# Placing the latent-attention products, four kept partial sums and the weight order of the gated output stage in a decoder block

## The chip, the core and the metric

One Trainium2 chip, one core of it. The metric is device time in microseconds of one execution: the median of the runs, beside one execution that the hardware profiler recorded. Engines are named as the profile names them: PE (TensorE, matrix products), PEld (its weight loads), DVE (VectorE), ACT (ScalarE), POOL (GpSimd), SP (the queue from which nearly all transfers are issued).

## The reference

One layer of a decoder block, batch 1, 1024 positions, width 1024, float32. Cut to what matters here:

```python
h    = rmsnorm(x, mix_norm_g)
proj = h @ w_in   # -> qa, ka, va (sliding window), q_lat (384), kv_lat (256), k_r (32), g_a, g_b (1024 each)
o_a  = swa_sink_attention(rope(qa), rope(ka), va, sinks)        # 8 heads of 64, window 128
qb   = rmsnorm(q_lat) @ w_uq      # 8 heads x (64 nope + 32 rope)
kvb  = rmsnorm(kv_lat) @ w_ukv    # 8 heads x (64 k_nope + 64 v)
o_b  = causal_softmax((q_nope k_nope' + rope(q_rope) rope(k_r)') * 96**-0.5) @ v
y    = sigmoid(g_a) * (o_a @ w_o_swa) + sigmoid(g_b) * (o_b @ w_o_mla)
x    = x + y @ w_out
x    = x + (silu(h2 @ w_gate) * (h2 @ w_up)) @ w_down           # h2 = rmsnorm(x)
out  = rmsnorm(x)
```

## The kernel before

Every matrix product is kept exact to nearly float32 by three products of two halves: an operand is split into a high part and the rest (`split`, L161: ACT copies the high part, DVE or POOL subtracts to get the low part), and `mm3` (L168) issues high·high, high·low, low·high at L172, L173 and L174. In the profile most matmuls therefore carry one of these three lines and most splits L163 (ACT) and L166 (DVE), so one goes by tile names.

The program has these stages: input projection and sliding-window attention with the gate products (`gate_step`) between, until about 347 us; then the **product stage** (loop at L1290), which makes from the latents `cq` and `ckv` the queries (`prod_q`, `prod_rope`), keys (`prod_k`) and values (`prod_v`) of the eight latent-attention heads; then the **head loop** over 64 steps t (L1326), eight heads of eight query blocks; then the **output stage** (`mix_b`, loop at L1394); then the product with `w_out` (tile `xo`, L1579) and the feed-forward part.

*Product stage.* For j in 0..3 it computes two 512-wide halves of `prod_k(j)` (6 matmuls each, heads 2j and 2j+1), for j<2 `prod_rope(j)` (18 matmuls, tiles `qr`, `qrs`), two halves of `prod_q(j)` (9 each) and two `prod_v` (6 each): 204 matmuls. Keys and queries are split, stored to DRAM (`kn_d`, `qn_d`, `qr_d`) and loaded again per head into the tiles `kT` (three of them, `load_k`, L1135) and `qT` (`load_q`, L1138), since a head's 64 rows and its rope rows have to lie in one tile of 96 partitions. Scores of steps 0 and 1 are issued within j = 3 (L1308, L1312).

*Head loop.* At step t the program issues `scores(t+2)` (PE products into a PSUM tile `scb`, DVE mask and row minimum at L1175, ACT exponential at L1176 into `p`, POOL reciprocal and scaling at L1177 and L1178), then the products with the values that are due (`pv`, L1214 and L1215, from three steps after their transposes on), then from t = 9 on a piece of the sliding-window output product `mix_a` (`fill`, L1321: 4 pieces of 6 matmuls in a head, tile `oA`), then `transposes(t)` (L1192, tile `pTb`, split into `pth` and `ptl`). Beside that, `split_oa` (L1236) splits the sliding-window output (`oar`) in steps 0 to 7. `mix_a(dc)` (L1253) leaves its 128 rows of `o_a @ w_o_swa` in a tile `ar`, stores it to `ar_d` and drops it (L1265 to L1267).

*Output stage.* For each of eight 128-row blocks dc of y: `load_sigs(dc)` loads two gate tiles (`sg`) and `ar`; `sigmoids` on ACT (L1248); `mix_b` (L1367): POOL multiplies `ar` by its gate (L1374), PE computes two halves of `o_b @ w_o_mla` (24 matmuls, tile `oB`), DVE multiplies them by the other gate (L1379), DVE adds one half and POOL the other (L1382, shown as L180), and `split` writes `yh` and `yl`. The weights `("ob", i)` serve the blocks 2i and 2i+1. They are loaded (`st.load_to`) before block 2i-2 and split into `wh`, `wl` (`st.conv_to`) after `mix_b` of block 2i-1, that is just ahead of their use:

```python
    for dc in range(8):
        ...
        if dc % 2 == 0 and dc < 6:
            st.load_to(st.index[("ob", dc // 2 + 1)])
        ...
        mix_b(dc)
        if dc % 2 == 1 and dc < 6:
            st.conv_to(st.index[("ob", dc // 2 + 1)])
```

*What sets the order.* From L1039 to L1557 nothing is ordered by hand: a planner in the compiler takes the instructions by program order as their priority, puts each engine's into one fixed list by its own cost estimates and reuses tile slots as they come free. Each engine and each queue then works its list in order; a waiting instruction holds all behind it. Tiles come from 21 slots "u" (4 KB per partition), 17 slots "v" (8 KB) and eight PSUM banks: four tiles `P1` and, in the other four banks, tiles `PX` (four of 512 columns, or two of 1024 in the head loop).

Of the kernel before, what the change touches and what calls it, by code (L numbers as in the profile page):

```python
# [8 lines left out]
F32 = mybir.dt.float32  # L9
F32R = mybir.dt.float32r  # L10
# [7 lines left out]
P = 128  # L18
# [71 lines left out]
def hybrid_block_kernel(  # L90
# [53 lines left out]
    def U(name, dt=F32, shape=(P, 1024)):  # L144
        return pool.tile(list(shape), dt, tag="u", name=uid(name))
# [7 lines left out]
    def P1(name, shape=(P, 512)):  # L153
        return ps1.tile(list(shape), F32, tag="ps", name=uid(name))
# [6 lines left out]
    def split(hi, lo, src, eng=None):  # L161

        i = nc.scalar.copy(hi, src)  # L163
        if held[0]:
            tc.keep_in_program_order(i)
        (eng or nc.vector).tensor_tensor(lo, src, hi.bitcast(F32), op=ALU.subtract)  # L166
# [18 lines left out]
    def half(s):  # L185
        return slice(512 * s, 512 * s + 512)
# [23 lines left out]
    ar_d = dram.tile([8, P, S], F32, name="ar_d")  # L210
# [87 lines left out]
    uq_unit(2)  # L298
    for dp in range(4):
        plain(("oa", dp), w_o_swa[dp], (P, 4, 256), True)  # L300
    for dp in range(4):
        plain(("ob", dp), w_o_mla[dp], (P, 4, 256))
    for r, hf in enumerate((0, 1, 0)):
        for j in range(4):
# [783 lines left out]
    wuq = st.get(("uq", 1)) + st.get(("uq", 2))  # L1088

    vM = []  # L1090
    qT = {}
    mask = U("mask")
    cos_t, sin_t = rope_t

    def prod_rope(s):
        ps = [P1("q") for _ in range(2)]
        for w, p in zip(w_rope, ps):
            mm3(p, [((w[:, 0, k], w[:, 1, k]), (cq[k][0][:, half(s)], cq[k][1][:, half(s)])) for k in range(3)])
        c, d = U("qr", F32, (P, 2, 512)), U("qr", F32, (P, 2, 512))
        for i in range(2):  # L1100
            nc.vector.tensor_tensor(c[:, i], ps[i], cos_t[:, half(s)], op=ALU.mult)
            nc.vector.tensor_tensor(d[:, 1 - i], ps[i], sin_t[:, half(s)], op=ALU.mult)
        sub(c[:, 0], c[:, 0], d[:, 0], nc.gpsimd)
        add(c[:, 1], c[:, 1], d[:, 1], nc.gpsimd)
        for i in range(2):
            t = U("qrs", F32R, (P, 2, 512))
            split(t[:, 0], t[:, 1], c[:, i], nc.gpsimd)
            nc.sync.dma_start(qr_d[i][:, :, half(s)], t.bitcast(F32))

    def prod_q(j, s):  # L1110
        w = wuq[j]
        ps = P1("q")
        mm3(ps, [((w[:, 0, k], w[:, 1, k]), (cq[k][0][:, half(s)], cq[k][1][:, half(s)])) for k in range(3)])
        t = U("qns", F32R, (P, 2, 512))
        nc.scalar.activation(t[:, 0], ps, AF.Copy, scale=-SC_B)
        nc.vector.scalar_tensor_tensor(t[:, 1], ps, -SC_B, t[:, 0].bitcast(F32), op0=ALU.mult, op1=ALU.subtract)
        nc.sync.dma_start(qn_d[j][:, :, half(s)], t.bitcast(F32))

    def prod_k(j, s):
        ps = P1("k")  # L1120
        mm3(ps, [((wk[0][:, k, blk(j)], wk[1][:, k, blk(j)]), (ckv[k][0][:, half(s)], ckv[k][1][:, half(s)]))
                 for k in range(2)])
        t = U("kns", F32R, (P, 2, 512))
        split(t[:, 0], t[:, 1], ps)
        nc.sync.dma_start(kn_d[j][:, :, half(s)], t.bitcast(F32))
# [10 lines left out]
        nc.sync.dma_start(kT[h % 3][0:64].bitcast(F32), kn_d[h // 2, 64 * (h % 2):64 * (h % 2) + 64])  # L1136

    def load_q(h):  # L1138
        t = qT[h] = V("qT", F32R, (P, 2, S))
        nc.sync.dma_start(t[0:64].bitcast(F32), qn_d[h // 2, 64 * (h % 2):64 * (h % 2) + 64])  # L1140
# [139 lines left out]

    wo = {}
    NT = NH * NB

    def load_sigs(dc):
        for i in (dc, 8 + dc):
            load_sig(i)
        ar[dc] = U("ar")
        nc.sync.dma_start(ar[dc], ar_d[dc])

    for j in range(4):  # L1290
        prod_k(j, 0)
        prod_k(j, 1)
        if j < 2:
            prod_rope(j)
        if j == 2:
            nc.vector.memset(mask[:, 0:S - P], 0.0)
            nc.vector.tensor_scalar(mask[:, S - P:], band[:, P:], -1.0, None, op0=ALU.mult)
        prod_q(j, 0)
        if j == 1:
            load_k(0)  # L1300
        if j == 2:
            load_k(1)
            load_q(0)
        if j == 3:
            load_k(2)
            load_q(1)
            psum_phase("psb", 2)
            scores(0)  # L1308
        prod_q(j, 1)
        prod_v(2 * j)  # L1310
        if j == 3:
            scores(1)  # L1312
        prod_v(2 * j + 1)
        if j == 1:
            for g in range(2):
                load_oa(g, 0)
        if j == 3:
            for g in range(2):
                load_oa(g, 1)
    st.load_to(st.index[("oa", 0)])  # L1320
    fill = {}  # L1321
    for i in range(16 - 2):
        for c in range(2):
# [2 lines left out]
    for t in range(NT):  # L1326
        h, n = divmod(t, NB)
        if t + 2 < NT:
            scores(t + 2)
        while pvq and pvq[0][0] <= t:  # L1330
            pv(*pvq.pop(0)[1:])
        if n == 2 and h + 2 < NH:
            load_q(h + 2)
        if n == 6 and h + 3 < NH:
            load_k(h + 3)
        hh, nn = step(t)
        if nn % 2 == 1:
            pvq.append((t + 3, hh, nn // 2))
        e = t - (NT - 8)
        if e == 6:  # L1340
            psum_phase("psc", 4)
        if t in fill:
            dc, sh, c0 = fill[t]
            mix_a(dc, sh, c0, 2, P1("oA") if c0 == 0 else None)
        transposes(t)
        held[0] = True
        if t < 8:
            split_oa(t % 4 // 2, t // 4, t % 2)
        if t == 4:
            st.conv_to(st.index[("oa", 0)])  # L1350
        if n in (0, 4) and h in (2, 4, 6):
            (st.load_to if n == 0 else st.conv_to)(st.index[("oa", h // 2)])
        if e == 4:
            load_sigs(0)
# [9 lines left out]
    for r in rest[1:]:  # L1364
        mix_a(*r, 0, 4, PX("oA"))

    def mix_b(dc):  # L1367
        if dc % 2 == 0:
            wo["b"] = st.get(("ob", dc // 2))
        w = wo["b"]  # L1370
        ga, gb = gate.pop(dc), gate.pop(8 + dc)
        a_ = ar.pop(dc)
        for sh in range(2):
            nc.gpsimd.tensor_tensor(ga[:, half(sh)], a_[:, half(sh)], ga[:, half(sh)], op=ALU.mult)  # L1374
        for sh in range(2):
            cs = half(sh)
            pb = PX("oB")
            mm3(pb, [((w[0][:, c, blk(dc % 2)], w[1][:, c, blk(dc % 2)]), obT[(c, sh)]) for c in range(4)])
            nc.vector.tensor_tensor(gb[:, cs], pb, gb[:, cs], op=ALU.mult)  # L1379
        for sh in range(2):  # L1380
            cs = half(sh)
            add(ga[:, cs], ga[:, cs], gb[:, cs], (nc.vector, nc.gpsimd)[sh * (dc < 7)])  # L1382
# [11 lines left out]
    for dc in range(8):  # L1394
        if dc + 2 < 8:
            load_sigs(dc + 2)
        if dc % 2 == 0 and dc < 6:
            st.load_to(st.index[("ob", dc // 2 + 1)])
        if dc + 1 < 8:
            sigmoids(dc + 1)  # L1400
        mix_b(dc)
        if dc % 2 == 1 and dc < 6:
            st.conv_to(st.index[("ob", dc // 2 + 1)])
        if dc >= 4:
            st.load_to(st.index[("out", 0, dc - 4)])
        if dc >= 5:
            st.conv_to(st.index[("out", 0, dc - 5)])
    st.conv_to(st.index[("out", 0, 3)])


# [149 lines left out]
    for seg, (sh, hf) in enumerate(((0, 0), (0, 1), (1, 1), (1, 0))):  # L1560
# [6 lines left out]
        for b in range(4 * sh, 4 * sh + 4):  # L1567
# [256 lines left out]
```

## Time and profile before

| | us |
|---|---|
| median of 3 runs (1368.16 to 1372.61) | 1369.6 |
| the profiled execution, whole | 1365.05 |
| its span, first to last instruction | 1363.2 |
| PE busy (modelled, matmuls overlap) | 1332.9 |
| DVE / ACT / POOL busy | 898.6 / 634.7 / 577.9 |
| mean granted PE clock | 0.991 |
| moved by the transfers | 232.01 MB, 170 GB/s |

A line of the time view reads: start, duration, engine, line of the kernel, operation, output tile <- input tiles, shape, and in brackets how long the engine was idle ahead of it and what ended that. A line of the stage view ("windows") gives for each engine the busy time in a stretch with the number of instructions, then the granted PE clock (1.00 is full), the mean busy share of the 16 DMA engines and their rate.

### The profile page before, as it was taken

Reading aid. Unit: us, or ns where it says so; the run is one execution under the profiler, and the core shown is the slowest. Engines: PE = TensorE matmul, PEld = TensorE weight load, DVE = VectorE, ACT = ScalarE, POOL = GpSimd, SP = SyncE. Lnnn points to the kernel's source line nnn. Section 1 sums busy time; section 2 is a strip of 40 time slices with the busy share of each in tenths; the row PEclk is TensorE's granted clock in tenths of the full one; section 3 lists DMA queues with packets and bytes.
Section 4 is the critical chain, followed back from the end, with each engine's and each line's share of the span. In section 5 each row is a group of like instructions: output and inputs, shape, how many; then the busy total and the mean of one; then the engine's idle time right before and its main releaser. Section 6 shows DMA issues by size and latency. Waiting matters only on the chain.

```text
span 1363.2 us, 19047 instructions
## 1 busy us (share of the span) xinstructions
PE 1332.9 (98%) x6564; PEld 1120.6 (82%) x6564; DVE 898.6 (66%) x1458; ACT 634.7 (47%) x1289; POOL 577.9 (42%) x621
## 2 busy tenths in 40 slices
PE   9999999999989999988999999999999999999997
PEld 6899878878878988867887888888888888888886
DVE  7868777776657667656448956666556654664862
ACT  7435666675346667744326323223222332644443
POOL 2126546452225554462031465766665551022421
PEclk9999999999999999989999999999999999999999
DMA  9464322335695431492243344654444525996504
GB/s 370 150 194 154 117 96 77 120 104 189 226 331 134 94 86 48 174 388 101 82 196 132 116 173 144 232 185 164 149 152 162 175 81 182 378 383 244 170 11 144
DMA packets 87873, 232.01 MB, mean 170 GB/s; under 512 B 9889, under 2 KB 16545, under 8 KB 86433
## 3 DMA queue, kind: packets, MB, share of 16 engines
q1 hardware_dynamic: 86336, 228.43, 48.4%
q10 hardware_dynamic: 1440, 2.36, 0.5%
q8 instruction: 52, 0.85, 0.3%
q14 instruction: 45, 0.36, 0.1%
HBM read 155.92 MB, written 74.32 MB: 169 GB/s over the span
## 4 chain that ended last, share of the span: by engine, by line
PE 86%; DVE 4%; issue 3%; POOL 3%; ACT 2%; DMA 1%; POOLq 0%; ACTq 0%; DVEq 0%
PE fa L174 7%; PE fa L172 7%; PE fa L173 7%; PE fb L174 6%; PE fb L172 6%; PE fb L173 6%; PE fd L172 5%; PE fd L174 5%; PE fd L173 5%; PE xo L173 2%; PE xo L174 2%; PE pTb L1192 2%; PE xo L172 2%; PE ob L1215 1%; PE ob L1214 1%
## 5 line engine op out<-in xcount | busy, mean ns | idle before, releaser
L166 DVE TENSOR_TENSOR wl<-wr,wl 128x512 fp32r<-128x512 f32 x150 | 151.9, 1037 | 72.1 <-ACT wl L163 71.8
L166 DVE TENSOR_TENSOR lrv<-lr,lrv 128x1024 fp32r<-128x1024 f32 x77 | 105.1, 1396 | 48.9 <-ACT lrv L163 45.0
L163 ACT CAST lrv<-lr 128x1024 fp32r<-128x1024 f32 x77 | 80.2, 1052 | 95.7 <-PE fd L174 59.5
L172 PE MATMUL fd<-lrv 128*128 128x512 f32 x308 | 119.8, 389 | 0.0
L173 PE MATMUL fd<-lrv 128*128 128x512 f32 x308 | 119.8, 389 | 0.0
L174 PE MATMUL fd<-lrv 128*128 128x512 f32 x308 | 119.8, 389 | 0.0
L177 POOL TENSOR_TENSOR wr<-wr,sm 128x512 f32<-128x512 f32 (+1 forms) x38 | 46.3, 1228 | 148.9 <-DVE wl L166 116.6
L163 ACT CAST wl<-wr 128x512 fp32r<-128x512 f32 x150 | 86.8, 622 | 1.4 <-DVE wr L831 1.2
L166 DVE TENSOR_TENSOR wl<-sm,wl 128x512 fp32r<-128x512 f32 x60 | 49.2, 846 | 46.4 <-ACT wl L163 46.3
L1177 POOL TENSOR_TENSOR denb<-denb,neg_one 128x1 f32<-128x1 f32 x64 | 39.2, 612 | 93.0 <-ACT p L1176 88.1
L310 POOL TENSOR_SCALAR ms<-ss 128x1 f32<-128x1 f32 x32 | 8.4, 263 | 144.3 <-ACT xn L1586 67.7
L174 PEld LDWEIGHTS fd<-lrv 128*128 128x128 f32 x308 | 57.8, 188 | 12.1
L173 PEld LDWEIGHTS fd<-lrv 128*128 128x128 f32 x308 | 57.8, 188 | 12.1
L172 PEld LDWEIGHTS fd<-lrv 128*128 128x128 f32 x308 | 57.8, 188 | 11.8
L1176 ACT ACTIVATE p<-scb,nmb 128x384 f32<-128x384 f32 (+3 forms) x64 | 47.8, 746 | 39.5 <-DVE nmb L1175 35.4
L166 DVE TENSOR_TENSOR ptl<-pTb,pth 128x512 fp32r<-128x512 f32 (+2 forms) x96 | 50.6, 553 | 22.1 <-ACT pth L163 21.4
L1175 DVE CUSTOM_DVE_ANT_0 scb<-scb,mask 128x384 f32<-128x384 f32 (+3 forms) x64 | 48.6, 761 | 17.9 <-PE scb L1167 15.9
L1478 ACT ACTIVATE act<-sm 128x512 f32<-128x512 f32 x11 | 7.0, 633 | 104.9 <-DVE sm L180 104.9
L1178 POOL TENSOR_SCALAR p<-p,denb 128x384 f32<-128x384 f32 (+3 forms) x64 | 49.1, 768 | 6.3
L172 PE MATMUL xo<-wv,yh 128*128 128x512 f32 x120 | 47.4, 395 | 2.2 <-ACT wv L163 2.2
L173 PE MATMUL xo<-wv,yh 128*128 128x512 f32 x120 | 46.8, 390 | 1.7 <-DVE wv L166 1.7
L1192 PE MATMUL pTb<-ident,p 128*128 128x128 f32 x288 | 43.8, 279 | 3.9 <-POOL p L1178 3.8
(352 smaller groups left out, 4296.8 us busy)
## 6 DMA issues: line engine op xcount, KB each, us to landing
lr<-la_d SPq DMA_DIRECT2D x77, 256.0 KB, 5.4
wr<-in_w_gate_dram SPq DMA_DIRECT2D x22, 512.0 KB, 4.1
wr<-in_w_up_dram SPq DMA_DIRECT2D x22, 512.0 KB, 5.2
wd<-in_w_down_dram SPq DMA_DIRECT2D x22, 512.0 KB, 6.8
rb_d<-wd SPq DMA_DIRECT2D x22, 512.0 KB, 2.7
la_d<-sd SPq DMA_DIRECT2D x22, 512.0 KB, 4.8
lr<-rb_d SPq DMA_DIRECT2D x44, 256.0 KB, 5.4
lr<-in_w_down_dram SPq DMA_DIRECT2D x33, 256.0 KB, 5.6
```

The source lines that it names most:

```text
L163: i = nc.scalar.copy(hi, src)
L166: (eng or nc.vector).tensor_tensor(lo, src, hi.bitcast(F32), op=ALU.subtract)
L172: nc.tensor.matmul(ps, ah, bh, start=first and i == 0, stop=False, skip_group_check=go_on)
L173: nc.tensor.matmul(ps, ah, bl, start=False, stop=False, skip_group_check=go_on)
L174: nc.tensor.matmul(ps, al, bh, start=False, stop=last and i == n - 1, skip_group_check=go_on)
L177: eng.tensor_tensor(out, a, b, op=ALU.subtract)
L1175: nc.vector.tensor_tensor_reduce(s_, s_, m_, 1.0, -NEG, op0=ALU.add, op1=ALU.min, accum_out=nm)
L1176: nc.scalar.activation(p_, s_, AF.Exp, scale=-1.0, bias=nm, accum_out=den)
L1177: nc.gpsimd.tensor_tensor(den, den, neg_one[:, 0:1], op=ALU.pow)
L1178: nc.gpsimd.tensor_scalar(p[:, 0:w], p[:, 0:w], den, 0.0, op0=ALU.mult, op1=ALU.add)
L1192: nc.tensor.transpose(pp[:, i], p[:, blk(k0 + i)], ident)
L1214: nc.tensor.matmul(po[:, q_off:], vst, hi[:, kb % 4, q_off:], start=kb == 0, stop=False)
```

## The change

Four parts.

1. The product stage is written out in another order. `prod_k(0)`, both `prod_rope`, `prod_q(0)`, `prod_k(1)`, `prod_q(1)` and the values come first, then `prod_k(2)`, `prod_q(2,0)`, `scores(0)`, `prod_q(2,1)`, a value block, `scores(1)`, two value blocks. `prod_k(3)` and `prod_q(3)` (30 matmuls) go into steps 0, 1, 2, 3, 5 and 6 of the head loop (`first`). Keys and queries of heads 0 and 1 are written by ACT and DVE straight into `kT` and `qT` in two pieces of 64 partitions, not through DRAM. `prod_rope` splits in place and stores high and low parts; it and `prod_q(0)`, `prod_q(1)` use the `PX` banks.
2. `load_oa`, the load of the first `w_o_swa` unit, its split and `split_oa` move into the steps 1 to 11 of the head loop.
3. `mix_a` of blocks 4 to 7 leaves its result in two "v" tiles that stay until the output stage; `ar_d` holds only blocks 0 to 3.
4. The output stage takes the blocks in the order 4, 0, 5, 1, 6, 2, 3, 7 and the `("ob", i)` units in the order 2, 0, 3, 1, two at a time; the first two are loaded in the last head. The `w_out` units are loaded one block earlier in the loop, and the `xo` product adds up its eight parts in a matching order.

The diff, cut:

```diff
     def prod_q(j, s, k0=0, n=3):
...
+        outs = [(t[:, 0], t[:, 1], ps)] if j else [
+            (qT[u][0:64, 0, half(s)], qT[u][0:64, 1, half(s)], ps[64 * u:64 * u + 64]) for u in range(2)]
...
     def prod_k(j, s):
...
+        if j == 0:
+            for u in range(2):
+                split(kT[u][0:64, 0, half(s)], kT[u][0:64, 1, half(s)], ps[64 * u:64 * u + 64])
+            return
...
     def mix_a(dc, sh, c0, n, ps=None):
...
-            ar[dc] = U("ar")
+            if dc < 4:
+                ar[dc] = U("ar")
+            elif dc % 2 == 0:
+                t = V("ar", F32, (P, 2, S))
+                ar[dc], ar[dc + 1] = t[:, 0], t[:, 1]
...
-            if sh == 1:
+            if sh == 1 and dc < 4:
                 nc.sync.dma_start(ar_d[dc], ar.pop(dc))
...
+    DCS = (4, 0, 5, 1, 6, 2, 3, 7)
...
+    prod_k(2, 0)
+    prod_k(2, 1)
+    prod_v(4)
+    load_k(2)
+    prod_q(2, 0)
+    psum_phase("psb", 2)
+    scores(0)
+    prod_q(2, 1)
+    prod_v(5)
+    scores(1)
+    prod_v(6)
+    prod_v(7)
+    first = {0: lambda: prod_k(3, 0), 1: lambda: prod_k(3, 1), 2: lambda: prod_q(3, 0, 0, 2),
+             3: lambda: prod_q(3, 0, 2, 1), 5: lambda: prod_q(3, 1, 0, 2), 6: lambda: prod_q(3, 1, 2, 1)}
...
+        if t in first:
+            first[t]()
...
-        if t < 8:
-            split_oa(t % 4 // 2, t // 4, t % 2)
-        if t == 4:
+        if t in (1, 5):
+            for g in range(2):
+                load_oa(g, t // 4)
+        if t == 3:
+            st.load_to(st.index[("oa", 0)])
+        if 4 <= t < 12:
+            split_oa(t % 4 // 2, t // 4 - 1, t % 2)
+        if t == 7:
             st.conv_to(st.index[("oa", 0)])
...
+        if e in (2, 6):
+            st.load_to(st.index[("ob", 2 if e == 2 else 0)])
         if e == 6:
-            st.conv_to(st.index[("ob", 0)])
+            st.conv_to(st.index[("ob", 2)])
...
+    sigmoids(DCS[0])
+    st.conv_to(st.index[("ob", 0)])
     new_quads("y")
+    for i, dc in enumerate(DCS):
+        if i in (1, 2):
+            st.load_to(st.index[("ob", (3, 1)[i - 1])])
+        if 3 <= i < 7:
+            st.load_to(st.index[("out", 0, i - 3)])
+        if i + 2 < 8:
+            load_sigs(DCS[i + 2])
+        if i + 1 < 8:
+            sigmoids(DCS[i + 1])
+        mix_b(dc, i)
+        if i in (2, 3):
+            st.conv_to(st.index[("ob", (3, 1)[i - 2])])
+        if i >= 4:
+            st.conv_to(st.index[("out", 0, i - 4)])
...
-            mm3(ps, [(hT(k, blk(b)), (wo2[k // 2][0][:, k % 2], wo2[k // 2][1][:, k % 2])) for k in range(NK)])
+            mm3(ps, [(hT(k, blk(b)), (wo2[k // 2][0][:, k % 2], wo2[k // 2][1][:, k % 2])) for k in (0, 1, 4, 5, 2, 6, 3, 7)])
```

More of the change, by code (lines that the diff above doesn't have):

```diff
@@ L1090, in hybrid_block_kernel @@
     vM = []
-    qT = {}
+    qT = {h: V("qT", F32R, (P, 2, S)) for h in range(2)}
     mask = U("mask")
@@ L1105, in prod_rope, with prod_q @@
         for i in range(2):
[L1106 to L1110, printed above, removed]
-        w = wuq[j]
[L1112 to L1117, printed above, removed]
+            split(d[:, i].bitcast(F32R), c[:, i].bitcast(F32R), c[:, i], nc.gpsimd)
+        for i, t in enumerate((d, c)):
+            nc.sync.dma_start(qr_d[:, :, i, half(s)].rearrange("a p c -> p a c"), t)
+    q_ps = {}
+    def prod_q(j, s, k0=0, n=3):
+        w = wuq[j]
+        if k0 == 0:
+            q_ps[0] = (P1 if j > 1 else PX)("q")
+        ps = q_ps[0]
+        mm3(ps, [((w[:, 0, k], w[:, 1, k]), (cq[k][0][:, half(s)], cq[k][1][:, half(s)])) for k in range(k0, k0 + n)],
+            k0 == 0, k0 + n == 3)
+        if k0 + n < 3:
+            return
+        t = U("qns", F32R, (P, 2, 512)) if j else None
+        outs = [(t[:, 0], t[:, 1], ps)] if j else [
+            (qT[u][0:64, 0, half(s)], qT[u][0:64, 1, half(s)], ps[64 * u:64 * u + 64]) for u in range(2)]
+        for hi, lo, src in outs:
+            nc.scalar.activation(hi, src, AF.Copy, scale=-SC_B)
+            nc.vector.scalar_tensor_tensor(lo, src, -SC_B, hi.bitcast(F32), op0=ALU.mult, op1=ALU.subtract)
+        if j:
+            nc.sync.dma_start(qn_d[j][:, :, half(s)], t.bitcast(F32))
     def prod_k(j, s):
@@ L1286, in load_sigs @@
             load_sig(i)
[L1287 to L1320, printed above, removed]
+        if dc < 4:
+            ar[dc] = U("ar")
+            nc.sync.dma_start(ar[dc], ar_d[dc])
+    prod_k(0, 0)
+    prod_k(0, 1)
+    prod_rope(0)
+    prod_rope(1)
+    prod_q(0, 0)
+    prod_q(0, 1)
+    prod_v(0)
+    load_q(0)
+    load_q(1)
+    prod_k(1, 0)
+    prod_k(1, 1)
+    prod_q(1, 0)
+    prod_q(1, 1)
+    prod_v(1)
+    prod_v(2)
+    prod_v(3)
+    nc.vector.memset(mask[:, 0:S - P], 0.0)
+    nc.vector.tensor_scalar(mask[:, S - P:], band[:, P:], -1.0, None, op0=ALU.mult)
+    prod_k(2, 0)
[12 more added lines that the diff above has]
+             3: lambda: prod_q(3, 0, 2, 1), 5: lambda: prod_q(3, 1, 0, 2), 6: lambda: prod_q(3, 1, 2, 1)}
     fill = {}
@@ L1387, in sigmoids @@
             sigmoid(i)
-    load_sigs(1)
+    load_sigs(DCS[1])
     split_ob(3, 0)
     split_ob(3, 1)
-    sigmoids(0)
+    sigmoids(DCS[0])
+    st.conv_to(st.index[("ob", 0)])
     new_quads("y")
[L1394 to L1407, printed above, removed]
+    for i, dc in enumerate(DCS):
[12 more added lines that the diff above has]
+            st.conv_to(st.index[("out", 0, i - 4)])
     st.conv_to(st.index[("out", 0, 3)])
```

23 lines of the change are left out of this document (13 added, 10 removed).

## The prediction

> **What bounds the kernel now.** I read the page first, then the busy times by stage, then the time view of PE wherever a stage showed PE short of full, then the other engines there.
>
> ```profile
> span 1363.2 us, 19047 instructions
> PE 1332.9 (98%) x6564; PEld 1120.6 (82%) x6564; DVE 898.6 (66%) x1458; ACT 634.7 (47%) x1289; POOL 577.9 (42%) x621
> ```
>
> PE is the bound, so a change pays only where PE is idle or slowed. The stages show where that is (start and end, then per engine busy us, PE clock, transfer share):
>
> ```profile
> 347.00:394.00 47.00, 46.90 (x206) 38.19 (x204) 22.03 (x35) 14.75 (x27) 10.17 (x8) 1.00 0.81 259
> 394.00:402.00 8.00, 5.71 (x28) 4.28 (x28) 5.50 (x12) 4.78 (x11) 3.27 (x6) 1.00 1.07 347
> 402.00:410.00 8.00, 6.64 (x32) 6.35 (x32) 6.92 (x16) 5.98 (x14) 4.71 (x7) 0.58 1.03 324
> 410.00:422.00 12.00, 9.95 (x65) 8.50 (x64) 10.19 (x22) 8.66 (x20) 7.25 (x8) 0.99 0.96 211
> 422.00:442.00 20.00, 20.00 (x135) 18.18 (x134) 13.84 (x32) 13.61 (x32) 10.22 (x17) 1.00 0.31 90
> ...
> 581.00:595.00 14.00, 8.08 (x21) 5.67 (x20) 6.83 (x7) 7.47 (x9) 10.95 (x8) 0.63 1.02 410
> 595.00:613.00 18.00, 17.84 (x79) 14.37 (x77) 11.18 (x13) 7.58 (x10) 9.99 (x7) 1.00 0.98 370
> 613.00:622.00 9.00, 5.03 (x14) 3.43 (x13) 7.42 (x8) 6.02 (x8) 4.42 (x3) 0.81 0.84 292
> ```
>
> Two places leak. The first head (394 to 422) loses 2.29 + 1.36 + 2.05 = 5.7 us of idle time, and 6.64 x 0.42 = 2.8 us to the clock of 0.58: **8.5 us**. The later heads (422 to 442) lose nothing. The product stage ahead (347 to 394) is full on PE. The output stage leaks from 581 to 622; its loss is counted below. The change touches just these places.
>
> **Part 1: products into the first head.** PE's gaps there, in the time view (in brackets the idle time and its end):
>
> ```profile
> 347.20 0.39 PE L172 MATMUL k<-ckv,wv 128*128 128x512 f32 x1
> ...
> 358.08 0.39 PE L172 MATMUL v<-wv,ckv 128*128 128x512 f32 x1
> ...
> 394.87 0.41 PE L1165 MATMUL scb<-kT,qT 96*128 96x384 f32 x1 [0.93 <-DMA qT<-qr_d]
> ...
> 397.05 0.50 PE L1165 MATMUL scb<-kT,qT 96*128 96x512 f32 x1 [0.72 <-ACT p L1176]
> ...
> 402.72 1.22 PE L1192 MATMUL pTb<-ident,p 128*128 128x128 f32 x7 [1.20 <-POOL p L1178]
> ...
> 417.66 0.66 PE L1192 MATMUL pTb<-ident,p 128*128 128x128 f32 x4 [1.93 <-POOL p L1178]
> ...
> 421.89 0.40 PE L172 MATMUL oA<-wv,wv 128*128 128x512 f32 x1
> ```
>
> From the first row to the second lie 48 matmuls (12 for keys, 36 for queries): 10.88 / 48 = **0.2267 us** each. The gaps end on softmax (ACT, POOL): a step of the first head has too little PE work to cover that latency, for no `mix_a` piece and few `pv` are due. The change puts 30 x 0.2267 = 6.8 us of products there, taken from a stage where each costs its full time. If they filled idle time only, and the clock held, the head would give back its 8.5 us; nothing else there can be gained. Against that stand lumps: `prod_k(3)` comes as 1.36 us in one step, and steps 4 and 7 get none. I keep one gap of the size of the 417.66 row, 2.0 us, and take **6.5**; the ends are 8.5 and, if the products only push softmax back, 0.
>
> The splits on DVE and ACT (mean ns after the busy time):
>
> ```profile
> L166 DVE TENSOR_TENSOR wv<-oar,wv 128x512 fp32r<-128x512 f32 x8 | 6.2, 774 | 0.2
> L163 ACT CAST wv<-oar 128x512 fp32r<-128x512 f32 x8 | 5.1, 636 | 0.0
> L166 DVE TENSOR_TENSOR vM<-v,vM 128x512 fp32r<-128x512 f32 x2 | 1.3, 684 | 0.0
> L163 ACT CAST vM<-v 128x512 fp32r<-128x512 f32 x2 | 1.1, 604 | 0.0
> ```
>
> Four product splits enter the head, 4 x (0.68 + 0.60) = 5.1 us; four of the eight `split_oa` leave it for steps 8 to 11, 4 x (0.77 + 0.64) = 5.6 us. That cancels; in the next head DVE is at 13.84 of 20 us and takes 4 x 0.77. Writing heads 0 and 1 in 64-row pieces adds four splits, again 5.1 us, in the product stage, where DVE is busy 22 of 47 us and ACT 15: cost 0 under PE; 5.1 at most without that cover. Moving load and split of the `w_o_swa` unit costs 0 by the same slack.
>
> Scores(0) comes earlier: 147 matmuls precede it in program order, 347.2 + 147 x 0.2267 = 380.5. Its keys and plain queries are then in place; its rope rows still go through DRAM:
>
> ```profile
> 358.25 2.55 POOL L166 TENSOR_TENSOR qrs<-qr,qrs 128x512 fp32r<-128x512 f32 x2 [0.73 <-ACT qrs L163]
> ```
> ```profile
> qr_d<-qrs SPq DMA_DIRECT2D x4, 512.0 KB, 3.1
> ...
> qT<-qr_d SPq DMA_DIRECT2D x9, 128.0 KB, 10.6
> ```
>
> The first rope half is done at 360.8 as now; the second, directly behind it on POOL, needs four such operations (5.1 us): 366. Store 3.1, issue about 2, load 10.6: 382, 1.5 us behind scores(0). The load is queued on SP after both stores, ahead of the stores of `prod_k(1)` and `prod_q(1)`, whose readers come heads later. 27 matmuls (6.1 us) stand between and behind scores(0) and scores(1), which the planner can put first. Cost 0; without that cover 1.5.
>
> **Part 2: the output stage.**
>
> ```profile
> 570.26 0.39 PE L172 MATMUL oB<-obT,wh 128*128 128x512 f32 x1
> ...
> 586.04 0.79 PE L172 MATMUL oB<-obT,wh 128*128 128x512 f32 x1 [4.74 <-ACT wh L163]
> ...
> 588.45 0.79 PE L174 MATMUL oB<-obT,wl 128*128 128x512 f32 x1 [1.19 <-DVE wl L166]
> ...
> 615.51 0.50 PE L172 MATMUL xo<-wv,yh 128*128 128x512 f32 x1 [2.23 <-ACT wv L163]
> 617.76 0.50 PE L173 MATMUL xo<-wv,yh 128*128 128x512 f32 x1 [1.74 <-DVE wv L166]
> ...
> 621.80 0.39 PE L172 MATMUL xo<-wv,yh 128*128 128x512 f32 x1
> ...
> 631.12 0.39 PE L173 MATMUL xo<-wv,yh 128*128 128x512 f32 x1
> ```
>
> Between the first and the last row lie 8 x 24 = 192 `oB` matmuls and four of `xo` (the first at 615.51, the last at 621.80): 196 x 0.2267 = 44.4 of 60.9 us. **16.4 us** are lost, idle time and the slow clock after it. What the 586.04 row waited for, on DVE, POOL, ACT, ACT, DVE:
>
> ```profile
> 581.76 0.68 DVE L1379 TENSOR_TENSOR sg<-oB,sg 128x512 f32<-128x512 f32 x1
> 582.61 1.78 POOL L180 TENSOR_TENSOR sg<-sg,sg 128x512 f32<-128x512 f32 x1 [1.32 <-ACT yh L163]
> 584.42 0.62 ACT L163 CAST yh<-sg 128x512 fp32r<-128x512 f32 x1 [0.92 <-POOL sg L180]
> 584.95 1.04 ACT L163 CAST wh<-wr 128x1024 fp32r<-128x1024 f32 x1
> 586.09 2.30 DVE L166 TENSOR_TENSOR wl<-wr,wh 128x1024 fp32r<-128x1024 f32 x1
> 601.29 1.22 DVE L166 TENSOR_TENSOR wl<-wr,wh 128x1024 fp32r<-128x1024 f32 x1
> ```
>
> The weight split ran on ACT without idle time ahead of it: it had not waited for its transfer but in line, behind the end of block 1, which itself follows PE's last matmul. So PE stood still for a whole chain: DVE, POOL, ACT, then the split. The change puts one block (24 x 0.2267 = 5.44 us of PE) between that split and its use. PE ended at 586.04 - 4.74 = 581.30; the high half was there at 585.99, 4.7 us later, the low half at 588.39, 7.1 later, or 6.0 with the 1.22 us of the 601.29 row. PE now wants them after 5.44 and, for the third matmul, 5.9. So the high half is in time and the low half 0.1 to 1.2 us late, for units 3 and 1: 0.2 to 2.4, I take 1.2. At the end, the new order of `xo` wants the last `w_out` unit after 15 matmuls (3.4 us) instead of 18; if its split stays behind block 7's chain (4.7) it is 1.3 late; I take 1.2. Gain 16.4 - 2.4 = **14.0**; the ends are 16.4 and 7 (below, second rival).
>
> [...]
>
> Transfers: sixteen of 512 KB are dropped (for each of `kn_d` and `qn_d` two stores and two loads, for `ar_d` four and four). In the output stage:
>
> ```profile
> sg<-gate_d SPq DMA_DIRECT2D x14, 512.0 KB, 10.2
> ar<-ar_d SPq DMA_DIRECT2D x7, 512.0 KB, 10.2
> ```
>
> 14 `sg`, 4 `ar`, 2 `ob` and 4 `w_out` are left, 24 x 0.524 MB = 12.6 MB, at the 410 GB/s of the 581 row 31 us under 44 us of PE. They do not bound. That the last `ar_d` store no longer holds SP is margin, not gain.
>
> **Sum.** 6.5 + 14.0 = 20.5 us. The profiled execution's own time is 1365.05 (1.85 beyond its span); it would be 1344.6. That execution lies 4.5 us under the median of 1369.6; I take the difference off the median: **1349**.
>
> A surcharge that I leave out: the clock of 0.58 in 402 to 410 followed gaps no longer than 1.2 us, so short gaps that stay may cost as much again, 2.8 us. [...]
>
> **Rivals.** *The first head gains nothing* (13 in 100): it is bound by softmax and DVE (6.92 of 8 us in 402 to 410), or the planner, for which program order is only a priority, puts the products back. 1369.6 - 14 = 1356. Against it: the DVE work cancels. *The weight splits stay in line* (13): the planner sets ACT's list by its own estimates and may put units 3 and 1 a block later still; half the gain, 1369.6 - 6.5 - 7 = 1356. Against it: the split at 601.29, for unit 2, cost PE no more than the 0.16 us that are missing in the 595 row. *Slots run out, slower* (12): two `ob` units at a time and gates two blocks ahead share the 21 "u" slots; a block holds three, so with fewer than nine free the gates of a block load only when another block is done, and each block lasts the 10.2 us of a load instead of 5.44. 8 x 10.2 = 82 us instead of 60.9: 1369.6 + 21 - 6.5 = 1384. Against it: I count 16 of 21 (6 `sg`, 2 `ar`, two `ob` units of 2 and 2 raw ones, 2 raw `w_out`). *No effect* (4): the planner undoes both placements, 1369.6.
>
> **Numbers.** The forecast has 58 in 100; faster in its case and the first two rivals (0.84), slower in the third (0.12), within 0.3% in the fourth (0.04); 0.3% is about what a measurement here can tell from no change. Range: from all 24.9 us, 1345, less 2 for scatter, 1343, up to both first rivals at once, 1369.6 - 7, 1362; the last two cases, 16 in 100, lie outside.
>
> **What would show it.** Right: no gap over 1 us on PE from 380 to 412 and clock 1.00 there; the first `oA` piece, last row of the first-head fence, near 415; no `oB` row waiting for `wh`, stage under 48 us. Wrong: gaps ended by `qT` or POOL in the first head, ACT's `wh` still behind `yh`, gates waiting for slots, or gaps in heads 2 to 8 from the two "v" slots held.

## The result and the profile after

The changed kernel takes **1354.75 us** (median of 4 runs, 1353.6 to 1357.95) beside 1370.1 of the kernel before; the ratio is 0.9891 with a 95% interval of 0.9866 to 0.9916, so by the ratio 14.9 us less (11.5 to 18.4). The forecast was 20.5 us less.

The head of the page of the changed kernel:

```profile
span 1356.1 us, 19021 instructions
...
PE 1332.1 (98%) x6564; PEld 1118.5 (82%) x6564; DVE 898.1 (66%) x1462; ACT 637.4 (47%) x1293; POOL 574.5 (42%) x621
```

The work is nearly the same on every engine (PE 1332.9 us before, DVE 898.6, ACT 634.7); what changed is when it runs. This profiled execution took 1357.95 us, above the median, and that of before 1365.05, below its median; the two spans differ by 7.1 us only. Nothing ahead of the first `k` matmul was changed, and yet it starts anywhere from 347.0 to 350.8 in the traces of all runs. So I don't subtract spans. I set each trace to the first `k`, where the changed code begins, and read three later marks: the first `oA`, the first `oB` and the last `xo` matmul with `wh`. PE's time view of the changed kernel:

```profile
350.56 0.39 PE L172 MATMUL k<-ckv,wv 128*128 128x512 f32 x1
...
383.88 0.34 PE L1182 MATMUL scb<-kT,qT 96*128 96x384 f32 x1
...
416.65 0.39 PE L172 MATMUL oA<-wv,wv 128*128 128x512 f32 x1
...
567.82 0.39 PE L172 MATMUL oB<-obT,wh 128*128 128x512 f32 x1
...
595.59 0.50 PE L172 MATMUL oB<-obT,wh 128*128 128x512 f32 x1 [0.41 <-ACT wh L163]
...
598.48 0.50 PE L174 MATMUL oB<-obT,wl 128*128 128x512 f32 x1 [2.15 <-DVE wl L166]
...
619.21 0.50 PE L172 MATMUL xo<-wv,yh 128*128 128x512 f32 x1 [1.07 <-ACT wv L163]
...
620.99 0.61 PE L173 MATMUL xo<-wv,yh 128*128 128x512 f32 x1 [1.28 <-DVE wv L166]
...
621.82 0.63 PE L172 MATMUL xo<-wv,yh 128*128 128x512 f32 x1
...
622.67 0.63 PE L174 MATMUL xo<-wv,yl 128*128 128x512 f32 x1
...
625.52 0.80 PE L172 MATMUL xo<-wv,yh 128*128 128x512 f32 x1 [2.22 <-ACT yh L163]
...
631.23 0.51 PE L173 MATMUL xo<-wv,yh 128*128 128x512 f32 x1
...
715.51 0.39 PE L172 MATMUL xo<-wh,yh 128*128 128x512 f32 x1
```

From `k` to the first `oA` before took 421.89 - 347.20 = 74.7 us and takes 66.1 now: 8.6 less. From `k` to the first `oB` it is 223.1 and 217.3: 5.8 less. Half of the 2.8 between the two is only the mark: 48 score matmuls (tile `scb`) lie between `k` and the first `oA` now, 54 before, so 6 x 0.2267 = 1.4 us of work went behind it; about 1.4 us are given back in heads 1 to 7. From there to the last `xo` (722.4 in the trace of before) it is 152.1 and 147.7: 4.4 less. The stall of 4.74 us for `wh` is gone, and later rows have smaller ones. The stages (start and end, then busy us per engine, PE clock, transfer share, rate):

```profile
394.00:410.00 16.00, 15.83 (x100) 13.68 (x99) 9.95 (x21) 10.55 (x25) 7.99 (x12) 1.00 0.72 213
410.00:422.00 12.00, 10.54 (x63) 8.58 (x62) 10.63 (x21) 8.32 (x18) 4.04 (x6) 1.00 0.97 285
...
581.00:595.00 14.00, 14.00 (x63) 11.42 (x61) 9.36 (x13) 8.11 (x11) 8.19 (x6) 1.00 0.56 203
595.00:613.00 18.00, 15.44 (x67) 12.17 (x67) 14.42 (x16) 8.77 (x11) 11.78 (x7) 1.00 0.90 315
613.00:622.00 9.00, 6.65 (x27) 4.93 (x26) 5.51 (x6) 4.10 (x5) 6.01 (x4) 0.96 0.17 70
622.00:635.00 13.00, 10.78 (x33) 8.06 (x32) 6.64 (x10) 5.64 (x7) 0.06 (x1) 0.64 0.00 1
```

The first head is full and at clock 1.00 from 394 to 410; from 410 to 422 PE still lacks 1.5 us. In the output stage the loss did not go away; it moved from 581 to 595 (5.9 us idle before, none now) to 595 to 635, into the last blocks. DVE's line shows why. It takes each half block of `oB` from PSUM at L1412:

```profile
570.74 0.69 DVE L1412 TENSOR_TENSOR sg<-oB,sg 128x512 f32<-128x512 f32 x1
...
626.11 0.68 DVE L1412 TENSOR_TENSOR sg<-oB,sg 128x512 f32<-128x512 f32 x1
```

PE ends the first half at 570.7 and DVE takes it at once. It ends the sixteenth at 614.7 (its last `oB` matmul starts at 614.35), and DVE takes that one at 626.11, 11.4 us late. DVE goes on by (626.11 - 570.74) / 15 = 3.69 us per half, 7.4 us per block, where PE needs 5.44. PE's waits name `wh`, `wl` and `wv`, but the splits that make them stand in the lines of ACT and DVE behind the ends of blocks (rows below, under the output stage). **The end of a block, not the order of the weights, has become the bound.** What makes it so long, DVE's work or its waits, the trace alone leaves open:

```profile
DVE yl L166 <- ACT yh L163: 17.4, 13, 2.5
...
ACT yh L163 <- POOL sg L180: 13.1, 7, 2.9
```

(Waits of the changed kernel from 567.8 to 631: the waiting instruction, what released it, us in total, times, longest.) DVE stands 17.4 us before `yl`; 7 of ACT's 16 `yh` wait for POOL's addition.

### The profile page after: what moved, and what is told of

Read it like the earlier page. It is cut to its first block, busy times and chain, and to the rows that moved or that the text cites. A ratio compares the mean times of both kernels' runs of the same rounds, so it can differ in the third digit from the quotient of the medians.

```text
span 1356.1 us, 19021 instructions
## 1 busy us (share of the span) xinstructions
PE 1332.1 (98%) x6564; PEld 1118.5 (82%) x6564; DVE 898.1 (66%) x1462; ACT 637.4 (47%) x1293; POOL 574.5 (42%) x621
## 4 chain that ended last, share of the span: by engine, by line
PE 83%; DVE 5%; issue 4%; POOL 4%; ACT 3%; DMA 1%; POOLq 0%; ACTq 0%; DVEq 0%
PE fa L174 7%; PE fa L172 7%; PE fa L173 7%; PE fb L174 6%; PE fb L172 6%; PE fb L173 6%; PE fd L173 5%; PE fd L174 5%; PE fd L172 5%; PE xo L172 2%; PE xo L173 2%; PE xo L174 2%; PE pTb L1209 2%; PE ob L1232 1%; PE ob L1231 1%
## 5 line engine op out<-in xcount | busy, mean ns | idle before, releaser
L172 PE MATMUL xo<-wv,yh 128*128 128x512 f32 x120 | 49.0, 408 | 3.3 <-ACT yh L163 2.2
L173 PE MATMUL xo<-wv,yh 128*128 128x512 f32 x120 | 48.3, 402 | 1.3 <-DVE wv L166 1.3
L174 PE MATMUL xo<-wv,yl 128*128 128x512 f32 x120 | 48.2, 402 | 0.0
```

The lines of the kernel that those rows point to most:

```text
L172: nc.tensor.matmul(ps, ah, bh, start=first and i == 0, stop=False, skip_group_check=go_on)
L173: nc.tensor.matmul(ps, ah, bl, start=False, stop=False, skip_group_check=go_on)
L174: nc.tensor.matmul(ps, al, bh, start=False, stop=last and i == n - 1, skip_group_check=go_on)
```

## Experiments

**Theories.** H: the stage is held by waits in line; DVE, which works in a fixed order, stands before `yl` until POOL has added and ACT has copied. C: it is held by longer rows; POOL's rows stretch DVE's rows that run beside them. Each experiment's times stand beside runs of the kernel before on the same chip (medians 1368.3 to 1369.5 us; 1370.1 beside the change). The marks are those of the section above, in us, from one profile each; the same program twice (4 and 11) has the same marks within 0.1 us:

| | median us | ratio to before (95%) | `k` to `oB` | `oB` to last `xo` |
|---|---|---|---|---|
| before | 1370.1 | 1 | 223.1 | 152.1 |
| the change | 1354.75 | 0.9891 (0.9866 to 0.9916) | 217.3 | 147.7 |
| 1 products only | 1360.03 | 0.9933 (0.9920 to 0.9947) | 217.0 | 151.7 |
| 2 output stage only | 1362.29 | 0.9951 (0.9933 to 0.9968) | 223.2 | 146.5 |
| 3 second half later | 1356.70 | 0.9910 (0.9896 to 0.9925) | 217.1 | 149.2 |
| 4 additions on DVE | 1347.29 | 0.9838 (0.9822 to 0.9854) | 217.2 | 139.1 |
| 5 before, additions on DVE | 1368.73 | 0.9997 (0.9988 to 1.0006) | 225.6 | 150.9 |
| 6 as 4, idle POOL addition | 1353.01 | 0.9888 (0.9875 to 0.9902) | 217.3 | 144.6 |
| 7 as 3, ACT's order turned | 1355.14 | 0.9903 (0.9887 to 0.9919) | 217.1 | 147.4 |
| 8 as 4, `oa` low halves on POOL | 1347.49 | 0.9846 (0.9831 to 0.9860) | 216.3 | 139.5 |
| 9 as 4, all `ar` stored | 1355.75 | 0.9903 (0.9886 to 0.9920) | 217.8 | 145.5 |
| 10 as 4, nothing on POOL | 1344.21 | 0.9822 (0.9809 to 0.9835) | 217.2 | 136.2 |
| 11 as 4, again | 1347.47 | 0.9845 (0.9831 to 0.9859) | 217.3 | 139.1 |
| 12 the change, all `ar` stored | 1358.01 | 0.9924 (0.9909 to 0.9939) | 217.8 | 148.9 |

**1 and 2: the two halves of the change alone.** Experiment 1 is the changed kernel with the output stage, the `ar` tiles and the weight order of before. Experiment 2 is the kernel before with the output part alone: order of blocks, weights and `xo` sum, earlier loads and the kept `ar` tiles. Of its edit:

```diff
     NT = NH * NB
+    DCS = (4, 0, 5, 1, 6, 2, 3, 7)
...
-    for dc in range(8):
+    for i, dc in enumerate(DCS):
```

> Only the products, their direct writes and the w_o_swa loads are moved; the output stage, its weight order and the eight stored ar blocks are those of before. Theory A (the traces of before and after, set to the start of the product stage: the first oA product comes 8.6 us earlier, the first oB product 5.8 us earlier): 5 to 7 us faster than before. Rival (the first head gives nothing lasting, all gain is in the output stage): within 2 us of before.

> Only the output stage is changed (block order, weight order, four kept ar blocks, earlier w_out loads, order of the xo sum); products and first head are those of before. Theory A (the output stage keeps 12.3 of its 16.4 us of PE loss, since the end of a block on DVE, POOL and ACT takes 7.5 us against 5.44 us of PE, and PE meets it a few blocks later): 3.5 to 6 us faster than before. Rival (the forecast's sizing): 14 us faster.

Measured: 9.2 us (7.3 to 11.0) and 6.7 us (4.4 to 9.2). They add up to 15.9, the change gave 14.9: within the intervals, two separate gains. The first is more than expected, the second under half of the 14 forecast. In experiment 2 the `wh` stall of 4.7 us is gone, in experiment 1 it is there (PE's time view of experiment 1):

```profile
580.90 0.79 PE L172 MATMUL oB<-obT,wh 128*128 128x512 f32 x1 [4.73 <-ACT wh L163]
```

So the output part removes this stall, and another limit stands behind it. Order and kept tiles came together here; experiment 12 takes them apart.

**3 and 7: the second half's split behind the next block's first product, by hand.** POOL's operations stay the same. Changed is the place at which DVE and ACT take up the second half; POOL's gate product comes one block earlier, and the order on these three engines is written by hand, not planned. In experiment 3 ACT copied the newer half first, in 7 the older one first (cut from 7):

```diff
             nc.vector.tensor_tensor(gb[:, cs], pb, gb[:, cs], op=ALU.mult)
+            if tail:
+                tail.pop(0)()
             add(ga[:, cs], ga[:, cs], gb[:, cs], (nc.vector, nc.gpsimd)[sh * (i < 7)])
...
+        tail.append(second_split)
```

> The changed kernel, with the work of the output stage unchanged but set in another order by hand on DVE, ACT and POOL: the split of a block's second half stands behind the next block's first product, and the gate product with ar one block earlier. Theory A (waiting in line: DVE stands idle for ACT and POOL within a block): blocks follow at about 5.5 us, the loss of 12.3 us falls to 2 to 4, and the kernel is 7 to 10 us faster than the changed one, 18 to 25 faster than before. Rival B (DVE and POOL have too much work in the stage, or hold each other up): no more than 2 us off the changed kernel.

> The kernel with the change, POOL's additions kept, with the second half's split put behind the next block's first product by hand, as in the earlier run, but now with ACT's copy of the older half ahead of that of the newer half. Theory H: the 1.26 us per block that DVE waited for yh in the earlier run goes (7 blocks, 9.1 us), the second half's addition has 2.7 us of cover: 1347 to 1351. Rival C: DVE's weight splits stay at 2.3 us beside POOL's gate products (1.22 alone) and hold PE: 1354 to 1357.

Measured: 1356.7 and 1355.1, both level with the change. DVE's wait before `yl` fell from 17.4 to 9.1 and then to 2.5 us, as H wanted, while that before `wl` rose from 1.0 to 4.1 and 4.6; no time came of it. The DVE rows of experiment 7 from 566.6 to 631 say where it went (line, operation, shapes, count, busy us, mean ns, idle time before):

```profile
L180 DVE TENSOR_TENSOR sg<-sg,sg 128x512 f32<-128x512 f32 x9 | 13.0, 1447 | 0.1
...
L166 DVE TENSOR_TENSOR wv<-wr,wv 128x1024 fp32r<-128x1024 f32 x5 | 8.4, 1671 | 0.8 <-ACT wv L163 0.8
```

An addition takes 1.45 us here and 0.98 in the changed kernel, a weight split 1.67 and 1.21. Most of the wait was traded for longer rows beside POOL. H alone does not explain the time.

**4 and 11: both additions of a block on DVE.**

```diff
-            add(ga[:, cs], ga[:, cs], gb[:, cs], (nc.vector, nc.gpsimd)[sh * (i < 7)])
+            add(ga[:, cs], ga[:, cs], gb[:, cs], nc.vector)
```

> The changed kernel with both additions of a block on DVE, none on POOL. Theory A (a chain of waits): the chain of a block loses the step to POOL and back, 1.3 to 2.1 us there against 0.7 to 1.1 on DVE, about 1 us a block; 3 to 6 us faster than the changed kernel. Rival B (too much work on DVE): DVE gets 7 more additions, 5 us, and the kernel is 3 to 6 us slower than the changed one. Rival C (POOL has too much work): as A or more, with DVE still waiting for nothing but PE.

> The kernel with the change and with all additions on DVE, once more, beside these two: every theory expects 1347.3 us within 1.5 us.

Measured: 1347.29, and 1347.47 in the repeat: about 7 us faster than the change, though DVE, the busy engine, got seven more operations. Either theory allows that: a wait for POOL is gone, and so are seven POOL rows of 1.69 us beside DVE's.

**6: an addition on POOL that nobody uses.** Experiment 4 with POOL's operation put back in the same place, into a tile that is no longer needed:

```diff
+            if sh == 1 and i < 7:
+                add(a_[:, cs], a_[:, cs], gb[:, cs], nc.gpsimd)
             add(ga[:, cs], ga[:, cs], gb[:, cs], nc.vector)
```

> The kernel with the change and with all additions on DVE (1347.3 us), plus one POOL addition of the same size and place as the one that was taken away, whose result nobody uses. Theory H (what cost time was that DVE and ACT wait in line for POOL's addition): nothing waits for this one but a slot, so the time stays within 2 us of 1347.3, and DVE's waits for yh stay near 2 us. Rival C (what cost time was POOL reading and writing memory beside DVE, which stretched DVE's rows): DVE's rows of two operands grow again, and the time goes back to 1353 to 1356.

Measured: 1353.0, 5.5 us (stage rows: 144.6 - 139.1) of the 8.6 between experiment 4 and the change. No row of PE, DVE or ACT waits for POOL in the stage. SP does once, 5.3 us for a slot, but no engine waits for a load there. DVE's rows in experiment 4 (566.8 to 622):

```profile
L180 DVE TENSOR_TENSOR sg<-sg,sg 128x512 f32<-128x512 f32 x16 | 15.1, 945 | 0.9
L166 DVE TENSOR_TENSOR yl<-sg,yh 128x512 fp32r<-128x512 f32 x16 | 14.1, 881 | 3.5 <-ACT yh L163 2.1 <-DMA wr<-in_w_o_mla_dram 0.7
...
L166 DVE TENSOR_TENSOR wv<-wr,wv 128x1024 fp32r<-128x1024 f32 x5 | 6.1, 1214 | 0.0
L166 DVE TENSOR_TENSOR wl<-wr,wh 128x1024 fp32r<-128x1024 f32 x3 | 4.7, 1580 | 1.0 <-ACT wh L163 1.0
```

and in experiment 6 (564.3 to 629):

```profile
L180 DVE TENSOR_TENSOR sg<-sg,sg 128x512 f32<-128x512 f32 x16 | 17.7, 1109 | 0.9
L166 DVE TENSOR_TENSOR yl<-sg,yh 128x512 fp32r<-128x512 f32 x16 | 14.9, 928 | 3.5 <-ACT yh L163 2.9
L166 DVE TENSOR_TENSOR wv<-wr,wv 128x1024 fp32r<-128x1024 f32 x6 | 8.4, 1397 | 0.0
L166 DVE TENSOR_TENSOR wl<-wr,wh 128x1024 fp32r<-128x1024 f32 x3 | 5.8, 1941 | 1.0 <-ACT wh L163 1.0
```

The same operations are longer by 16 x 0.164 + 16 x 0.047 + 6 x 0.183 + 3 x 0.361 = 5.6 us, which is the time lost. That DVE's line sets the end of the stage is in PE's last wait there, in experiment 4 and in 6:

```profile
619.13 0.50 PE L174 MATMUL xo<-wv,yl 128*128 128x512 f32 x1 [0.56 <-DVE yl L166]
```
```profile
622.16 0.50 PE L174 MATMUL xo<-wv,yl 128*128 128x512 f32 x1 [0.56 <-DVE yl L166]
```

From the first `oB` (566.82 and 564.28) these are 52.3 and 57.9 us, again 5.6 more. This shows C: an operation that nobody waits for costs as much as it stretches DVE. The other 3.1 us (147.7 - 144.6) are left for the waits of H; that is what remains of a difference, not a measurement of its own.

**10: nothing on POOL.** Experiment 4 with the gate products on DVE too:

```diff
-            nc.gpsimd.tensor_tensor(ga[:, half(sh)], a_[:, half(sh)], ga[:, half(sh)], op=ALU.mult)
+            nc.vector.tensor_tensor(ga[:, half(sh)], a_[:, half(sh)], ga[:, half(sh)], op=ALU.mult)
```

> The kernel with the change and with all additions on DVE (1347.3 us), and now the products of the gate with the local part on DVE as well (16 rows of 128x512 more), so that POOL does nothing in the output stage. Theory C (POOL's rows stretch DVE's): DVE's rows come back to 0.68 to 0.69 us for 128x512 and 1.22 us for 128x1024 throughout, so its work in the stage grows only from 52.9 us to some 55.6 us (64 x 0.685 + 8 x 1.22 + 2): 1 to 4 us slower than the repeat run. Rival (the long rows come from something other than POOL, a transfer or ACT): they stay at 0.88 to 0.95 us, DVE's work grows to some 67 us: 8 to 12 us slower.

Measured: 1344.21, 3.3 us *faster* than the repeat beside it, each of its runs below each of the repeat's. DVE's rows, 565 to 629:

```profile
L166 DVE TENSOR_TENSOR yl<-sg,yh 128x512 fp32r<-128x512 f32 x16 | 10.8, 689 | 0.1
L180 DVE TENSOR_TENSOR sg<-sg,sg 128x512 f32<-128x512 f32 x16 | 10.7, 689 | 0.1
L1407 DVE TENSOR_TENSOR sg<-ar,sg 128x512 f32<-128x512 f32 x14 | 9.4, 688 | 0.0
L166 DVE TENSOR_TENSOR wv<-wr,wv 128x1024 fp32r<-128x1024 f32 x7 | 8.5, 1221 | 0.0
L166 DVE TENSOR_TENSOR wl<-wr,wh 128x1024 fp32r<-128x1024 f32 x3 | 3.7, 1222 | 0.8 <-ACT wh L163 0.8
```

Every row of 128x512 is back at 0.69 us and every weight split at 1.22, as C said, though the transfers' share is 0.83 (row below), so it isn't they that stretch DVE: with `L1412` (10.8) and two `obT` rows (1.3) the work is 55.2 us, where 55.6 was expected. The time that I drew from it had the wrong sign. DVE's total was never the price by itself; what counts is whether its rows are done when PE wants them. Now they are:

```profile
566.00:609.00 43.00, 43.00 (x191) 35.61 (x190) 41.01 (x63) 30.11 (x38) 0.00 (x0) 1.00 0.83 322
```

PE runs 43 us without a gap, DVE at 41.0 of these 43. There is little to spare: DVE takes the fourteenth half 5.9 us after PE has ended it (610.08, 604.19), and PE then waits once, 0.51 us at 613.76. The stage is 152.1 - 136.2 = 15.9 us shorter than before, nearly the 16.4 that the prediction had as the ceiling. This is the fastest version: 0.9822 (0.9809 to 0.9835), faster than both kernels.

**5: the addition alone, on the kernel before.** The edit of experiment 4 without the change.

> The kernel before with one edit: in each block of the output stage the second half's addition is made on DVE, not on POOL. Theory H (the stage is held by an in-order line: DVE's subtraction yl waits for ACT's yh, which waits for POOL's addition, and ACT's weight copies stand behind yh): in the kernel before, DVE waited 11.8 us for yh in this stage, of which some 7 in the second halves, and ACT's wh came 4.7 us late behind a yh; 5 to 9 us faster than before, so the new weight order would not be needed for such a gain. Rival N (the addition matters only once the weights come earlier, because in the kernel before the first stall, 4.73 us for wh, stands by the order of the issue): within 2 us of before.

Measured: no difference (0.9988 to 1.0006). DVE's wait for `yh` fell from 11.8 to 4.9 us, but PE still waits for the weights (waits of experiment 5, 575.7 to 640):

```profile
DVE yl L166 <- ACT yh L163: 4.9, 7, 0.7
PE oB L172 <- ACT wh L163: 4.9, 2, 4.5
```

The rival was right. The same edit is worth nothing behind the weights' stall and 7 us once the stall is gone. (`k` to `oB` is 2.5 us longer than before with the same PE work in the same order: this profile has a second stretch of half clock, 0.51 from 420 to 427.)

**12 and 9: the kept `ar` tiles undone,** on the change itself and on experiment 4:

```diff
-            if dc < 4:
-                ar[dc] = U("ar")
-            elif dc % 2 == 0:
-                t = V("ar", F32, (P, 2, S))
-                ar[dc], ar[dc + 1] = t[:, 0], t[:, 1]
+            ar[dc] = U("ar")
```

> The kernel with the change (1354.75 us, ratio 0.9891), POOL's additions as they are in it, with only its third part undone: all eight local products go through memory and come back. Theory T (the four transfers each way matter by themselves: with them the stage moves more than 400 GB/s throughout and ar comes late, as in the run with DVE's additions): 4 to 8 us slower than the kernel with the change, ratio 0.994 to 0.997. Rival S (here the end of each block on DVE and POOL lasts 7.5 us, longer than the transfers of a block, and hides them): within 2 us of the kernel with the change, ratio 0.988 to 0.990.

> The kernel with the change and with all additions on DVE (1347.3 us), with the third part of the change undone: all eight local products go through memory and come back, as in the kernel before. Theory (no engine waits for ar in this stage; its 4 transfers each way are hidden): within 1.5 us of the repeat run beside it. Rival T (the stage's transfers stand near the limit, 0.83 of 16 engines' time and 304 to 311 GB/s in 566 to 612, and the 2.1 MB more that come back push the weights behind them): 2 to 5 us slower than the repeat, with new waits for transfers in the stage.

Measured: 3.3 us more than the change (the intervals overlap, and the marks give 1.7), between both expectations; and 8.3 us more than the repeat of experiment 4, beyond what even the rival gave (6.9 by the marks). In experiment 9 the SP queue stands for the `ar_d` stores until ACT has made the last `ar` tiles (SP's waits, 540 to 640), and the loads behind them come late. The transfers fall to a share of 0.40 first and are then busy without a break (1.03):

```profile
SPq L1284 <- ACT ar L1282: 16.5, 2, 9.3
```
```profile
565.00:570.00 5.00, 4.51 (x24) 3.52 (x24) 2.69 (x4) 2.99 (x6) 0.55 (x1) 1.00 0.40 161
...
590.00:600.00 10.00, 7.23 (x25) 5.13 (x24) 7.77 (x11) 7.17 (x9) 3.43 (x3) 0.83 1.03 410
```

Its waits from 565 to 635 have a transfer among the first:

```profile
POOL sg L1402 <- DMA ar<-ar_d: 10.6, 2, 9.0
...
PE oB L172 <- ACT wh L163: 2.5, 1, 2.5
```

The load of that `ar` was issued at 569.84, right behind the store at 569.43, so the 9.0 us are the queue's doing as much as the transfers'; no run separates the stores from the bytes. How these delays reach the late `wh` step by step is argued, not shown. By these two runs the third part of the change is worth more where less else holds the stage. The new order alone, experiment 12 against experiment 1, is 1.2 us by ratio and not told from nothing, and with it alone the stall is back (PE in experiment 12):

```profile
593.34 0.79 PE L172 MATMUL oB<-obT,wh 128*128 128x512 f32 x1 [4.28 <-ACT wh L163]
```

So the order removes it only together with the kept tiles. What the kept tiles are worth with the old order, no run shows.

**8: what is given back in heads 1 to 7.** Experiment 4 with the low halves of `split_oa` on POOL.

> The kernel with the change and with all additions on DVE (1347.3 us), with the eight low halves of the first oa split (128x512 each) on POOL in place of DVE. If the 2.5 us that were given back between the first oA and the first oB piece came from DVE's load in the second head (8.0 of 8 us busy in one stretch, PE 0.5 to 1.5 us short in two), then 1 to 2.5 us faster: 1345 to 1346.5. Rival: POOL's normalisations of p in the same steps are pushed back by 1.3 to 2 us each and PE waits for them instead: the same or up to 3 us slower.

Measured: 1347.49, no difference; `k` to `oB` is 0.9 us shorter, of about 1.4 given back. The rest stays open.

## Why the prediction was right or wrong

**First head, forecast 6.5 of 8.5.** The mechanism held: no gap on PE from 380 to 411, clock 1.00, scores(0) at 383.88 with no wait on `qT` (33.3 us after `k`, as the 147 matmuls said). The "issue about 2" on the way to `qT` was an estimate; two such loads took SP 1.62 us in the trace of before (at 382.83), four 2.17 in that of the changed kernel (at 371.41). The step "I keep one gap of the size of the 417.66 row", 2.0 us, was about right. Ahead of the first `oA` three gaps stay, 1.5 us in all; they end on DVE now, not on softmax:

```profile
411.40 0.30 PE L1209 MATMUL pTb<-ident,p 128*128 128x128 f32 x1 [0.41 <-DVE ptl L166]
...
413.21 0.63 PE L1209 MATMUL pTb<-ident,p 128*128 128x128 f32 x4 [0.19 <-DVE ob L1243]
...
416.43 0.39 PE L1232 MATMUL ob<-ptl,vM 128*128 128x256 f32 x1 [0.86 <-DVE ptl L166]
...
424.04 0.52 PE L1209 MATMUL pTb<-ident,p 128*128 128x128 f32 x3 [0.34 <-DVE ptl L166]
```

So some 7.0 us were gained there (8.5 - 1.5); the 8.6 at the mark hold the 1.4 us of scores that went behind it. What was a little off is the 0 for `split_oa` in the next steps ("DVE is at 13.84 of 20 us and takes 4 x 0.77"): DVE is busy 8.00 of 8 us from 422 to 430, PE waits 0.34 us for it at 424.04, and experiment 8, with the low halves on POOL, is 0.9 us shorter. The net by the traces is 5.8, close to 6.5; by the medians the part alone gave 9.2 (7.3 to 11.0). The one trace of before was some 5 us under its median. Experiment 5 shows that this place varies in the kernel before: the same PE work, traced again, has a second half-clock stretch and takes 225.6 us to `oB`, 8.6 more than experiment 1. How often that comes, the traces don't show.

**Output stage, forecast 14.0 of 16.4.** Measured 4.4 by the traces, 6.7 alone by the median. This is the step that failed: "the high half was there at 585.99, 4.7 us later ... PE now wants them after 5.44". It took the 4.7 us from PE's last matmul to the split as a constant, measured at block 1. It is a lag that grows: DVE's line takes 7.4 us per block, waits included, PE 5.44, and the lag ends at 11.4. ACT still has unit 1's `wh` directly behind a `yh` (ACT's time view of the changed kernel):

```profile
593.97 0.63 ACT L163 CAST yh<-sg 128x512 fp32r<-128x512 f32 x1 [0.88 <-DVE sg L180]
594.50 1.04 ACT L163 CAST wh<-wr 128x1024 fp32r<-128x1024 f32 x1
```

In the kernel before, PE's stalls gave DVE time to catch up, so the lag there looked fixed: DVE takes the halves of `oB` up to 4.6 us late ahead of the stall at 615.51, and some 1.4 us late behind it. The residual was put at 2.4; by the traces it is 16.4 - 4.4 = 12.0. The rows name 0.41 + 2.15 + 1.07 + 1.28 + 2.22 = 7.1 of idle time, and the half clock from 621.2 to 631.5 some 3.5 more: 13 x (5.71 / 13 - 0.2267) = 2.8 behind the last of them (13 matmuls from 625.52 to 631.23) and 4 x (1.68 / 4 - 0.2267) = 0.8 ahead of it (620.99 to 622.67). The sign "stage under 48 us" came by its own count, 192 `oB` and four `xo` matmuls from 567.82 to 615.65, and misled: the loss sits mostly behind them. The rival "the weight splits stay in line" had the right price, 7, and half of the mechanism: one unit does stand in line, but because the end of the blocks is late; that the planner put it there too late, no row shows.

**Transfers, "they do not bound", "margin, not gain".** True of the forecast's own case, not of the stage. The count left out what else is due there: 8 `w_out` units, not 4, and 4 loads of `x`. And the store that holds SP was no mere margin: with all `ar` stored, SP stands for it until 569.43, inside the stage, and with DVE's additions the four kept tiles are worth 8.3 us.

**DVE's rows beside POOL.** The forecast of the output stage has a longer row in one place only: the low half of 2.30 us beside one of 1.22, which parts its ends of 1.2 and 0.1 us late, for two splits. Such rows were the main term: 5.5 us for seven additions on POOL, by experiment 6. Not every row grew: L1412, which reads PSUM and one SBUF tile, has 680, 681 and 690 ns in experiments 6, 4 and 10, while L180, with two SBUF inputs, has 1109, 945 and 689.

**Slots and planner.** Neither rival came: SP does wait for free slots in the output stage, but no engine there waits for a gate's load, and both placements stood.

**The whole.** 14.9 us instead of 20.5, 1354.75 instead of 1349, lies inside the range of 1343 to 1362, but nearer to the 1356 of two rivals that did not come as they were told. The output stage gave a third to a half of its 14; the range's width covers that, and so does a first part that by the medians gave 9.2 for 6.5. That part of the agreement is luck.

## What to carry to other kernels

When a stall is taken away, work out for each engine of that stage what it needs per block once nothing stalls, waits and stretched rows included; the slowest of these is the next bound, and a lag that was measured behind a stalled engine is not a constant (here DVE ended 11.4 us behind PE). Moving work to an idle engine was not free here, since seven additions on POOL made DVE's rows 5.6 us longer: compare the row's duration beside that engine and alone, and try the whole stage without it. Judge an edit of the second limit only after the first is gone; the same edit gave 0 and 7 us here.

## What the runs showed of the hardware that was not expected

- POOL additions of 1.8 us that nobody uses made DVE's rows longer by some 0.8 us each (5.6 us for 7), and the kernel by as much; DVE with all the elementwise work of the stage (0.69 us a row) was faster than the two together.
- The clock did not go by the length of a gap. In the changed kernel a gap of 2.15 us (the row at 598.48) left it at 1.00, and gaps of 1.07 and 1.28 us (619.21 and 620.99) were followed by the half clock, matmuls 0.43 us apart, before the gap of 2.22 us came. In experiments 4 and 11, the same program, the same matmul waited 1.80 and 1.83 us for `wl`; the stages behind it:

```profile
597.00:600.00 3.00, 3.00 (x15) 2.47 (x14) 2.90 (x4) 0.43 (x1) 0.53 (x1) 1.00 0.92 356
```
```profile
597.00:600.00 3.00, 3.00 (x8) 2.30 (x7) 2.84 (x4) 0.56 (x2) 0.40 (x1) 0.50 1.01 351
```

  By the granted clock, the half-clock stretches between 400 and 640 us lasted 6.83, 10.24 and 3.41 us in the kernel before (from 403.3, 584.2 and 618.4) and 10.24 us in the changed one (from 621.2). What decides whether one begins, no run tested.
